# Hybrid gMLP and RG-LRU layer: spatial product in two halves with both weight parts in one matmul, another order of the v tiles, sums moved between engines

## The chip, the cores and the metric

The kernel runs on one core of a Trainium2 chip. The metric is the device time of one execution in microseconds (us). A core has a matrix engine (TensorE, PE in the profile; its weight loads are listed apart as PEld), VectorE (DVE), ScalarE (ACT), GpSimd (POOL) and SyncE (SP), which here only issues transfers. They run their own streams of instructions and wait for each other through semaphores. TensorE writes its results to PSUM, eight banks of 2 KB per partition (512 fp32 numbers); everything else lives in SBUF, 128 partitions wide.

## The reference, cut to what matters

One layer of a decoder, 1024 prompt tokens and 8 samples (T = 1032 columns), width 1024:

```
h = rmsnorm(x, norm_g) * (1 + scale) + shift
u, v, g_a, x_b, g_b, z_a, z_b = split(h @ w_in)
v = rmsnorm(v, v_norm_g)
ws = tril(w_s[g])
s = einsum('gts,bnsgc->bntgc', ws, vp) + b_s
y_a = (u * s) * silu(g_a)
xc = conv(x_b, state_conv)
a = exp(-8 r softplus(-lam)),  h_t = a_t h_{t-1} + sqrt(1 - a_t^2) (i_t xc_t)
y_b = h * silu(g_b)
merged = sigmoid(z_a) * (y_a @ w_pa) + sigmoid(z_b) * (y_b @ w_pb)
out = x + gate * (merged @ w_out);  y = rmsnorm(out, final_g)
```

The spatial product is the line with the einsum: for each of 8 groups g of 128 channels and each of 8 chunks of 128 tokens, a 128 x 128 lower-triangular matrix times v, then v's norm weight and the bias b_s. The results are wanted at fp32 accuracy.

## The kernel before, in words

**Precision.** Every fp32 operand of a matmul is split into a rounded part (hi, by a copy on ScalarE) and the rest (lo, by a subtraction on VectorE). A product is the sum of three matmuls in the fast format: hi hi, hi lo and lo hi.

**Stages.** First come the modulation vectors, h and the projection to v (`v_tile`, line 677: 24 matmuls of 512 columns for one token tile and one half of the channels, into one PSUM bank; tile 8 is the samples, 41 weight columns wide). `v_evac` (line 669) copies the bank out on VectorE and sums its squares on ScalarE. Then the program changes to four pairs of PSUM banks (`new_phase(bufs=4)`, line 1427) and runs 24 units: R i, Z i and G i for i = 0 to 7, each a block of columns of w_in against h by a Strassen scheme of seven products p1 to p7 (`seven`, line 858; 24 matmuls of 258 columns each). The order of the products is p1, p6, p5, p2, p7, p3, p4, and p1, p4, p2, p6, p5, p7, p3 in the first unit. The sums of h that this needs are made by `x_forms(kp)` (line 757): for each of four kp, four sums on GpSimd, then four more sums on VectorE, each with a split into S1 to S4. In the products' names a_, b_, c_, d_ are the pairs of banks, s_, p_, u_ the copies out of them, wf_R1p7 the split weight form of product p7 of unit R1, wt_ and raw_ its sources.

After the units come the two projections (`pa`, `pb`, 344 columns a matmul), the output projection and the last norm.

**The order of the work.** From unit 1 on, every engine runs its instructions as the program writes them (`InOrder`, line 39; nearly every row of the profile is therefore put down to line 46, in the changed kernel 45). Work beside the products stands in a table: `at(n, ...)` (line 1452) puts a step behind product n of the run, counted over all units. For group g, `spatial(g, n)` (line 1492) takes n = the first product of unit G g (five products later for the last group). Ahead of G g stands R g+1, so n - 7 is that unit's p1, n - 4 its p2 and n - 3 its p7. `v_load` at n - 9 fetches v and w_s, `v_mask`, `v_wst` and `v_scale` at n - 7 make the transposed weight wsb and the scaled v, `v_hi` at n - 6 makes vnh, `v_lo` at n - 5 makes vnl (line 1049, one subtraction on VectorE), and `sp_mm` at n - 3 (line 1066) is the spatial product: 8 token tiles of three matmuls of 128 columns. Its result sp is taken up by VectorE in `fin` (four operations of 256 columns and a small one for the samples), which waits in the list `later` until the next product's matmuls are written.

**Around the first unit.** The tiles of v's second half run on PE in the order 4, 5, 6, 8 (line 717), then the phase changes, then 7 (line 1429), the form sums of kp 0 to 2 and the first weight forms, then 3 (line 1436) and the form sums of kp 3. `do_rgconsts` (line 1134) holds a chain of small operations on 8 columns for softplus(-lam): Abs and Exp on ScalarE (`le`), then `l`, `crg` and `ncrg` on VectorE.

Of the kernel before, what the change touches and what calls it, by code (L numbers as in the profile page):

```python
# [13 lines left out]
P = 128  # L14
# [10 lines left out]
HD = 512  # L25
NF = 2
EPS = 1e-6
EVAC_PRIO = 400
C_RG = 8.0
NSLOT = 36  # L30

# [23 lines left out]
def tile_hybrid_step(  # L55
# [102 lines left out]
        A.activation(hi, src, AF.Copy)  # L158
        (eng or V).tensor_tensor(lo, src, hi.bitcast(F32), ALU.subtract)

    last_w = [None]

    def load_raw(name, shape, parts):
        raw = wst[0].tile(shape, F32, tag="raw", name=f"raw_{name}", bufs=4)
# [52 lines left out]
        )  # L217
        return rs[:rows, :n]

    crow = sml.tile([72, P], F32, tag="rows", name="crow", bufs=5)  # L220
    nc.sync.dma_start(out=crow[0:64, :], in_=c_sample.rearrange("b (k p) -> (b k) p", p=P))
    nc.sync.dma_start(out=crow[64:72, :], in_=c_prompt.rearrange("b (k p) -> (b k) p", p=P))

# [89 lines left out]
    def vec_load(eng, parts):  # L313
        a = parts[0][0]
        e = parts[-1][0] + parts[-1][1].shape[0] // P
        vrow = sml.tile([e - a, P], F32, tag="rows", name=f"vrow{a}", bufs=5)
        for off, src in parts:
            if isinstance(src, tuple):
                c0 = src[2]
                with tc.issue_after(last_w[0]):  # L320
                    for q in range(2):
                        eng.dma_start(
                            out=vrow[off - a : off - a + KT, 64 * q : 64 * q + 64],
                            in_=src[q].rearrange("(k p) -> k p", p=P)[:, c0 : c0 + 64],
                        )
                continue
            n = src.shape[0] // P
            if eng is not G:
                with tc.issue_after(last_w[0]):
                    eng.dma_start(  # L330
                        out=vrow[off - a : off - a + n, :], in_=src.rearrange("(k p) -> k p", p=P)
                    )
                continue
            eng.dma_start(
                out=vrow[off - a : off - a + n, :], in_=src.rearrange("(k p) -> k p", p=P)
            )
        return vrow, a, e
# [331 lines left out]
    def v_evac(tt, half, ps):  # L669
        st = half_tile(f"vst{tt}_{half}")[:, 0:HD]  # L670
        V.tensor_copy(st, ps)
        A.activation(junk[:, 0:HD], ps, AF.Square, accum_out=ssv[:, tt, half : half + 1])
        nc.sync.dma_start(out=vd[tt * P : (tt + 1) * P, half * HD : (half + 1) * HD], in_=st)

    vsr = slot("vsr", [P, D])[0:NS]
# [38 lines left out]
        v_evac(tt, 0, vps[tt, 0])  # L714
    v_tile(3, 0)
    v_tile(8, 0)
    for tt in (4, 5, 6):
        v_tile(tt, 1)
    v_tile(8, 1)
    vss = ctile([P, 1], "vss")  # L720
    A.activation(junk[:NS], vsr, AF.Square, accum_out=vss[:NS])
# [5 lines left out]
    V.tensor_tensor(vsr, vsr, vgb, ALU.mult)  # L727
    nc.sync.dma_start(out=chunk_v_sample[0, :, 0, :], in_=vsr)

    vst = ctile([P, KT, NS], "vst")  # L730
    vgc = ctile([P, KT], "vgc")
    w00 = ctile([P, KT], "w00")

    def spatial_consts():
        ones1 = sml.tile([1, P], F32, tag="rows", name="ones1", bufs=5)
        G.memset(ones1, 1.0)
        vgr = sml.tile([KT, P], F32, tag="rows", name="vgr", bufs=5)
        w0r = sml.tile([1, KT], F32, tag="w0r", name="w0r", bufs=1)
        with tc.issue_after(last_w[0]):
            nc.sync.dma_start(out=vgr, in_=v_norm_g[0].rearrange("(k p) -> k p", p=P))  # L740
            nc.sync.dma_start(out=w0r, in_=w_s[0, :, 0, 0:1].rearrange("g o -> o g"))
        pst = consts_pair[:, 0]
        TE.matmul(pst[:, 80 : 80 + KT], ones1, w0r, start=True, stop=True)
        for k in range(KT):
            TE.transpose(
                pst[:, k * NS : (k + 1) * NS], vsr[0:NS, k * P : (k + 1) * P], ident[0:NS, 0:NS]
            )
        TE.transpose(pst[:, 64 : 64 + KT], vgr, ident[0:KT, 0:KT])
        rg_transposes()
        A.activation(w00, pst[:, 80 : 80 + KT], AF.Copy)  # L750
        A.activation(vst, pst[:, 0:64].rearrange("p (k b) -> p k b", k=KT), AF.Copy)
        A.activation(vgc, pst[:, 64 : 64 + KT], AF.Copy)
# [4 lines left out]
    def x_forms(kp):  # L757
        a11, a21 = h[kp, 0], h[kp, 1]
        a12, a22 = h[kp + 4, 0], h[kp + 4, 1]
        f1 = slots.tile([P, 2, HT], F32, tag="s", name=f"f1_{kp}")  # L760
        f2 = slots.tile([P, 2, HT], F32, tag="s", name=f"f2_{kp}")
        f3 = slots.tile([P, 2, HT], F32, tag="s", name=f"f3_{kp}")
        for dst, a in ((f1[:, 1], a21), (f2[:, 1], a22), (f1[:, 0], a11), (f2[:, 0], a12)):
            G.tensor_tensor(dst, a[:, 0].bitcast(F32), a[:, 1].bitcast(F32), ALU.add)

        def form(name, src):
            t = slots.tile([P, 2, HT], F32R, tag="s", name=f"{name}_{kp}")
            split(t[:, 0], t[:, 1], src)
            HF[name, kp] = t

        V.tensor_tensor(f3[:, 0], f1[:, 1], f2[:, 1], ALU.add)
        form("S1", f3[:, 0])
        V.tensor_tensor(f3[:, 1], f3[:, 0], f1[:, 0], ALU.subtract)
        form("S2", f3[:, 1])
        V.tensor_tensor(f1[:, 1], f1[:, 0], f1[:, 1], ALU.subtract)
        form("S3", f1[:, 1])
        V.tensor_tensor(f2[:, 0], f2[:, 0], f3[:, 1], ALU.subtract)
        form("S4", f2[:, 0])
        HF["A11", kp], HF["A12", kp], HF["A22", kp] = a11, a12, a22
# [231 lines left out]
    def v_load(g):  # L1011
        vg = slot(f"vg{g}", [P, NT, P])
        S.dma_start(
            out=vg,
            in_=vd[:, g * P : (g + 1) * P].rearrange("(n p) c -> p n c", p=P),
        )
        wsr = aux[0].tile([P, 2, P], F32, tag="c1", name=f"wsr{g}", bufs=2)
        S.dma_start(out=wsr[:, 0], in_=w_s[0, g])
        S.dma_start(out=wsr[:, 1], in_=b_s[0, g].partition_broadcast(P))
        vn[g] = {"v": vg, "w": wsr}  # L1020

    def v_mask(g):
# [40 lines left out]

        later.append(fin)

    def sp_mm(g):
        vnl, wsr, vnh, wsb = (vn[g][k] for k in "lwhb")
        bsb = wsr[:, 1]
        ps = pair_bank(f"sp{g}")
        for n in range(NT):  # L1070
            d = ps[:, n // 4, n % 4 * P : (n % 4 + 1) * P]
            for j, (v, w) in enumerate(((vnh, 0), (vnh, 1), (vnl, 0))):
                TE.matmul(d, v[:, n, :], wsb[:, w, :], start=(j == 0), stop=(j == 2))

        def fin():
            t3 = t3s[g] = slot(f"t3_{g}")
            bv = bsb.rearrange("p (o t) -> p o t", o=1).broadcast_to([P, 2, P])
            for b in range(2):
                for q in range(2):
                    V.scalar_tensor_tensor(  # L1080
                        q4(t3)[:, 2 * b + q, 0:QP].rearrange("p (j t) -> p j t", j=2),
                        ps[:, b, q * QP : (q + 1) * QP].rearrange("p (j t) -> p j t", j=2),
                        vgc[:, g : g + 1],
                        bv,
                        ALU.mult,
                        ALU.add,
                    )
            V.scalar_tensor_tensor(
                q4(t3)[:, :, QP:QW],
                vst[:, g, :].rearrange("p (q x) -> p q x", q=4),  # L1090
                w00[:, g : g + 1],
                bsb[:, 0:1].rearrange("p (o t) -> p o t", o=1).broadcast_to([P, 4, 2]),
                ALU.mult,
                ALU.add,
            )

        later.append(fin)

# [13 lines left out]
    rgrows = []  # L1112

    def load_rgconsts():
        strow = sml.tile([64, P], F32, tag="rows", name="strow", bufs=5)
        srow = [sml.tile([96, P], F32, tag="rows", name=f"srow{j}", bufs=5) for j in range(2)]
        scv = state_conv[0].rearrange("b w (k p) -> (b w k) p", p=P)
        with tc.issue_after(last_w[0]):
            nc.sync.dma_start(
                out=strow, in_=state_rglru_h[0].rearrange("b (k p) -> (b k) p", p=P)  # L1120
            )
            for j in range(2):
                nc.sync.dma_start(out=srow[j], in_=scv[j * 96 : (j + 1) * 96, :])
            nc.sync.dma_start(out=conv_sample[0, :, 0:2, :], in_=state_conv[0, :, 1:3, :])
        rgrows.extend([strow, srow])
# [8 lines left out]
    def do_rgconsts():  # L1134
# [14 lines left out]

        lamv = vec[:, V_LAM : V_LAM + KT]  # L1150
        le = ctile([P, KT], "le")
        A.activation(le, lamv, AF.Abs)
        A.activation(le, le, AF.Exp, scale=-1.0)
        l1 = ctile([P, KT], "l1")
        V.tensor_scalar(l1, le, 2.0, None, ALU.add)
# [147 lines left out]

    def do_states(_, w):
        pso = [bank(f"pso{j}") for j in range(2)]
        orow = [sml.tile([96, P], F32, tag="rows", name=f"orow{j}", bufs=5) for j in range(2)]
        ofv = ofm[:].rearrange("p q k -> p (q k)")
        for j, (a, n) in enumerate(((0, 96), (96, 64))):
            TE.transpose(pso[j][0:n, 0:P], ofv[:, a : a + n], ident)
# [116 lines left out]
    load_rgconsts()  # L1426
    new_phase(bufs=4)
    load_unit(units[0])
    v_tile(7, 1)
    for kp in range(3):  # L1430
        x_forms(kp)
    for n in range(4):
# [59 lines left out]
    def spatial(g, n):  # L1492

        at(n - 9, v_load, g)
        at(n - 7, v_mask, g)
        at(n - 7, v_wst, g)
        at(n - 7, v_scale, g)
        at(n - 6, v_hi, g)
        at(n - 5, v_lo, g)
        at(n - 3, sp_mm, g)  # L1500

    for i in range(KT):
        recurrent(i)
# [175 lines left out]
```

## Time and profile before

| | |
|---|---|
| median of 3 runs | 971.16 us (970.68 to 972.37) |
| the profiled execution | 969.83 us |
| its span from first to last instruction | 968.1 us |
| PE busy | 944.6 us, 6639 matmuls |
| VectorE busy | 628.0 us |
| ScalarE busy | 499.8 us |
| GpSimd busy | 232.4 us |
| mean granted clock | 0.996 |

The share of busy time is an average over the span. A row of the timeline gives the start and the length of an instruction, or of neighbours of one kind that are put together, and in brackets the idle time of its engine just before it with what ended it. Matmuls overlap in the rows: the time of a stretch of them is the difference of two starts, not the sum of the lengths. The profiled execution lies 1.33 us under the median.

### The profile page before, as it was taken

How to read it: one execution, taken by the hardware profiler on the slowest of the kernel's cores; microseconds unless marked ns; L12 is line 12 of the kernel's file. 1: busy time of each engine (PE TensorE's matmuls, PEld its weight loads, DVE VectorE, ACT ScalarE, POOL GpSimd, SP SyncE). 2: the span in 40 equal slices, each digit the busy share in tenths (PEclk: the TensorE clock that was granted, in tenths of full speed). 3: DMA queues.
4: the chain of work that ended last, by engine and by line, in shares of the span. 5: the costliest groups of instructions: out<-in, count | busy, mean ns of one | idle time of the engine just before them, and what ended most of it. 6: DMA issues, size and time to landing. Idle time of an engine off the chain costs nothing. (4 is left out here: it accounts for less than half of the span.)

```text
span 968.1 us, 16680 instructions
## 1 busy us (share of the span) xinstructions
PE 944.6 (98%) x6639; PEld 883.4 (91%) x6639; DVE 628.0 (65%) x969; ACT 499.8 (52%) x809; POOL 232.4 (24%) x173
## 2 busy tenths in 40 slices
PE   7999998999999999999999999998999999999996
PEld 3777768999999999999999999998999999998785
DVE  3888878568588496685774866868443366555544
ACT  4674444784775855847747558477122223232212
POOL 1142455242232342322422523331000000000001
PEclk9999999999999999999999999999999999999998
DMA  9953112243144162341431613417775465334321
GB/s 290 288 173 110 56 51 60 61 138 114 30 137 126 40 187 60 100 131 45 137 94 38 187 51 86 144 57 273 257 270 178 172 217 188 144 99 163 110 83 50
DMA packets 126790, 125.74 MB, mean 130 GB/s; under 512 B 10374, under 2 KB 104126, under 8 KB 126704
## 3 DMA queue, kind: packets, MB, share of 16 engines
q1 hardware_dynamic: 125496, 120.44, 38.7%
q0 software_dynamic: 1216, 4.24, 1.2%
q8 instruction: 52, 0.85, 0.4%
q14 instruction: 26, 0.21, 0.1%
HBM read 93.39 MB, written 31.33 MB: 129 GB/s over the span
## 5 line engine op out<-in xcount | busy, mean ns | idle before, releaser
L46 PE MATMUL v<-wv,h 128*128 128x512 f32 x384 | 97.2, 401 | 4.3 <-DVE h L46 1.8
L46 PE MATMUL ps_pb<-ybh,pb 128*128 128x344 f32 x384 | 92.4, 323 | 3.0 <-issue 3.0
L46 PE MATMUL ps_pa<-yah,pa 128*128 128x344 f32 x384 | 91.3, 320 | 0.0
L46 PEld LDWEIGHTS v<-wv,h 128*128 128x128 f32 x384 | 69.5, 188 | 22.5 <-DVE h L46 3.5
L46 POOL TENSOR_TENSOR rs_o<-ms_o,nhalf 128x1 f32<-128x1 f32 (+1 forms) x9 | 8.0, 894 | 299.0 <-DVE ms_o L46 299.0
L46 PEld LDWEIGHTS ps_pb<-ybh,pb 128*128 128x128 f32 x384 | 67.5, 191 | 3.2 <-issue 3.2
L46 PEld LDWEIGHTS ps_pa<-yah,pa 128*128 128x128 f32 x384 | 66.4, 188 | 0.5
L46 PE MATMUL ps_pb<-ybl,pb 128*128 128x344 f32 x192 | 62.1, 323 | 0.0
L46 PE MATMUL ps_pa<-yal,pa 128*128 128x344 f32 x192 | 61.3, 319 | 0.0
L46 PE MATMUL o<-woh,mgh 128*128 128x512 f32 x128 | 50.5, 395 | 0.0
L46 PE MATMUL o<-woh,mgl 128*128 128x512 f32 x128 | 50.5, 394 | 0.0
L46 PE MATMUL o<-wol,mgh 128*128 128x512 f32 x128 | 50.4, 394 | 0.0
L46 DVE SCALAR_TENSOR_TENSOR xc<-xb,vec,xc 128x512 f32<-128x512 f32 x48 | 44.2, 920 | 0.6
L46 ACT ACT_TABLE_LOAD x34 | 43.6, 1283 | 1.4 <-PEq L1663 0.8
L46 ACT ACTIVATE mgh<-sa 128x344 fp32r<-128x344 f32 x24 | 11.7, 490 | 62.6 <-DVE sa L46 58.8
L46 DVE TENSOR_TENSOR sb<-ps_pb,sb 128x344 f32<-128x344 f32 x24 | 12.4, 516 | 47.2 <-PE ps_pb L46 46.8
L46 ACT ACTIVATE junk<-xr 128x512 bf16<-128x512 f32 (+2 forms) x19 | 11.6, 608 | 56.8 <-DVE xr L46 51.4
L46 POOL TENSOR_TENSOR wt_R<-raw_R,raw_R 128x512 f32<-128x512 f32 x8 | 16.8, 2106 | 95.4 <-DVE wf_Z4p L46 13.7
L46 PEld LDWEIGHTS ps_pb<-ybl,pb 128*128 128x128 f32 x192 | 36.7, 191 | 0.0
L46 PEld LDWEIGHTS ps_pa<-yal,pa 128*128 128x128 f32 x192 | 36.1, 188 | 0.2
L46 ACT ACTIVATE r<-rg,vec 64x516 f32<-64x516 f32 x32 | 22.0, 687 | 26.9 <-PE rg L46 26.9
L46 POOL TENSOR_TENSOR wt_R<-raw_R,wt_R 128x512 f32<-128x512 f32 x15 | 32.8, 2184 | 8.6 <-DVE wf_R2p L46 1.1
(533 smaller groups left out, 2543.7 us busy)
## 6 DMA issues: line engine op xcount, KB each, us to landing
raw_ada<-in_w_ada_dram SPq DMA_DIRECT2D x32, 256.0 KB
raw_R<-in_w_in_dram SPq DMA_DIRECT2D x16, 512.0 KB
raw_Z<-in_w_in_dram SPq DMA_DIRECT2D x16, 512.0 KB
raw_G<-in_w_in_dram SPq DMA_DIRECT2D x16, 512.0 KB
zad<-za SPq DMA_DIRECT2D x16, 258.0 KB
yad<-t SPq DMA_DIRECT2D x8, 516.0 KB
sb<-zbd SPq DMA_DIRECT2D x8, 516.0 KB
yar<-yad SPq DMA_DIRECT2D x8, 516.0 KB
```

The lines of the kernel that those rows point to most:

```text
L46: ins = f(*args, **kwargs)
```

## The change

1. The spatial product of a group is cut into two halves of four token tiles, pr = 0 behind the product at n - 4 and pr = 1 behind the one at n - 3. For each tile, the two matmuls of vnh against w_hi and w_lo become one of 256 columns, whose two results of 128 columns are written 256 columns apart in one bank; the third, vnl against w_hi, adds to the second of them. VectorE takes a half up in two operations of 2 x 256 columns in place of two of 256, the second adding to what the first wrote; for this b_s is loaded twice (8 more transfers in all).
2. The tiles of v's second half run in the order 4, 8, 5, 6, 7, all ahead of the phase change, and 3.
3. The four sums of `x_forms(3)` move from GpSimd to VectorE.
4. The first operation on `le` is written to stand behind the last sum of squares of v on ScalarE.
5. `EVAC_PRIO` (not used), the number of buffers of `rows` (5 to 4) and the place of the tile `ones1`.

```diff
 def v_evac(tt, half, ps):
-        A.activation(junk[:, 0:HD], ps, AF.Square, accum_out=ssv[:, tt, half : half + 1])
+        last_a[0] = A.activation(
+            junk[:, 0:HD], ps, AF.Square, accum_out=ssv[:, tt, half : half + 1]
+        ).ins
...
-    for tt in (4, 5, 6):
-        v_tile(tt, 1)
+    v_tile(4, 1)
     v_tile(8, 1)
...
+    for tt in (5, 6, 7):
+        v_tile(tt, 1)
...
-            G.tensor_tensor(dst, a[:, 0].bitcast(F32), a[:, 1].bitcast(F32), ALU.add)
+            (G if kp < 3 else V).tensor_tensor(
+                dst, a[:, 0].bitcast(F32), a[:, 1].bitcast(F32), ALU.add
+            )
...
-        wsr = aux[0].tile([P, 2, P], F32, tag="c1", name=f"wsr{g}", bufs=2)
+        wsr = aux[0].tile([P, 3, P], F32, tag="c1", name=f"wsr{g}", bufs=2)
         S.dma_start(out=wsr[:, 0], in_=w_s[0, g])
-        S.dma_start(out=wsr[:, 1], in_=b_s[0, g].partition_broadcast(P))
+        for j in (1, 2):
+            S.dma_start(out=wsr[:, j], in_=b_s[0, g].partition_broadcast(P))
...
-    def sp_mm(g):
+    def sp_mm(g, pr):
         vnl, wsr, vnh, wsb = (vn[g][k] for k in "lwhb")
-        bsb = wsr[:, 1]
-        ps = pair_bank(f"sp{g}")
-        for n in range(NT):
-            d = ps[:, n // 4, n % 4 * P : (n % 4 + 1) * P]
-            for j, (v, w) in enumerate(((vnh, 0), (vnh, 1), (vnl, 0))):
-                TE.matmul(d, v[:, n, :], wsb[:, w, :], start=(j == 0), stop=(j == 2))
+        wcat = wsb[:].rearrange("p a t -> p (a t)")
+        ps = pair_bank(f"sp{g}_{pr}")
+        for b in range(2):
+            parts = ps[:, b, :].rearrange("p (a j t) -> p j a t", a=2, j=2)
+            for j in range(2):
+                n = pr * 4 + b * 2 + j
+                TE.matmul(parts[:, j], vnh[:, n, :], wcat, start=True, stop=False)
+                TE.matmul(parts[:, j, 1], vnl[:, n, :], wsb[:, 0, :], start=False, stop=True)
 
         def fin():
...
+            tv = q4(t3)[:, 2 * pr : 2 * pr + 2, 0:QP]
+            vg = vgc[:, g : g + 1]
+            V.scalar_tensor_tensor(tv, ps[:, :, QP : 2 * QP], vg, bv, ALU.mult, ALU.add)
+            V.scalar_tensor_tensor(tv, ps[:, :, 0:QP], vg, tv, ALU.mult, ALU.add)
...
-        A.activation(le, lamv, AF.Abs)
+        with tc.issue_after(last_a[0]):
+            A.activation(le, lamv, AF.Abs)
...
-    v_tile(7, 1)
...
-        at(n - 3, sp_mm, g)
+        at(n - 4, sp_mm, g, 0)
+        at(n - 3, sp_mm, g, 1)
```

The first place is PE in unit R1, around the spatial product of group 0. a_R, b_R and c_R are the banks of the unit's products; the first rows are the end of p2, the b_R rows are p7, the c_R row is the start of p3. Before:

```order
L46 MATMUL a_R_2324<-h_0_734,wf_R1p_2394 128x258 x3
L46 MATMUL b_R_2325<-S_0_1399,wf_R1p_2430 128x258 x3
...
L46 MATMUL sp_2505<-wsb_2390,vnh_2401 128x128 x2
L46 MATMUL sp_2505<-wsb_2390,vnl_2436 128x128
...
L46 MATMUL c_R_2326<-S_0_1403,wf_R1p_2464 128x258 x3
```

In the changed kernel:

```order
L45 MATMUL a_R_2325<-h_0_734,wf_R1p_2395 128x258 x3
L45 MATMUL sp_0_2470<-wsb_2391,vnh_2402 128x2x128
L45 MATMUL sp_0_2470<-wsb_2391,vnl_2437 128x128
...
L45 MATMUL b_R_2326<-S_0_1399,wf_R1p_2431 128x258 x3
...
L45 MATMUL sp_1_2519<-wsb_2391,vnh_2402 128x2x128
...
```

The first matmul that reads vnl stood behind all of p7; now it is the second instruction behind p2.

The second place is VectorE in unit R2, around the subtraction that makes vnl of group 1. Before:

```order
L46 TENSOR_TENSOR vnl1_3216<-vg1_3062,vnh1_3181 128x1024
L46 TENSOR_TENSOR wf_R2p3_3244<-raw_R2_1_2866,wf_R2p3_3244 128x512
L46 TENSOR_TENSOR wf_R2p4_3277<-wt_R2_3028,wf_R2p4_3277 128x512
...
L46 SCALAR_TENSOR_TENSOR t3_1_3336<-sp1_3285,vgc_1276,wsr1_3064 128x256 x4
```

In the changed kernel:

```order
L45 TENSOR_TENSOR vnl1_3211<-vg1_3056,vnh1_3176 128x1024
L45 TENSOR_TENSOR wf_R2p3_3239<-raw_R2_1_2860,wf_R2p3_3239 128x512
L45 SCALAR_TENSOR_TENSOR t3_1_3281<-sp1_0_3244,vgc_1305,wsr1_3058 128x2x256
L45 SCALAR_TENSOR_TENSOR t3_1_3281<-sp1_0_3244,vgc_1305,t3_1_3281 128x2x256
L45 SCALAR_TENSOR_TENSOR t3_1_3281<-vst_1304,w00_1306,wsr1_3058 128x4x2
L45 TENSOR_TENSOR wf_R2p4_3285<-wt_R2_3022,wf_R2p4_3285 128x512
```

vnl keeps its place on VectorE; the operations that take up the first half of sp now stand between the lo parts of the weight forms of p3 and p4.

The third place is ScalarE ahead of the first copy out of the first unit (s1_R0). Before:

```order
L46 ACTIVATE vgc_1276<-consts_1515 128x8
L46 ACTIVATE sth_1330<-consts_1515 128x256
L46 ACTIVATE S4_3_1512<-f2_3_1493 128x516
L46 ACTIVATE s1_R0_1650<-a_R0_1595 128x516
```

In the changed kernel:

```order
L45 ACTIVATE sth_1359<-consts_1515 128x256
L45 ACTIVATE junk_100,ssv_811<-v3_1_1463 128x512
L45 ACTIVATE le_1545<-vec_101 128x8
L45 ACT_TABLE_LOAD
L45 ACTIVATE le_1545<-le_1545 128x8
L45 ACTIVATE s1_R0_1650<-a_R0_1595 128x516
```

The two operations on `le` and a table load moved directly ahead of s1_R0; the 25 operations of the chain behind them moved with them on VectorE, in among the weight splits of the first unit.

## Rows read from the trace of the kernel before

**Rows 1.** The page: busy time, share of the span and instructions of each engine.

```profile
PE 944.6 (98%) x6639; PEld 883.4 (91%) x6639; DVE 628.0 (65%) x969; ACT 499.8 (52%) x809; POOL 232.4 (24%) x173
```

**Rows 2.** Waits of PE: waiting tile, releaser: us in total, times, longest.

```profile
PE ps_pb L46 <- issue: 3.0, 1, 3.0
...
PE a_R L46 <- ACT s_R L46: 1.6, 1, 1.6
PE v L46 <- DVE vsr L46: 1.4, 1, 1.4
PE b_R L46 <- ACT u_R L46: 1.3, 1, 1.3
```

**Rows 3.** Timeline of PE from 222 us, unit R1: start, length, instruction.

```profile
223.31 3.02 PE L46 MATMUL b_R<-S,wf_R1p 128*128 128x258 f32 x24
226.17 0.33 PE L46 MATMUL sp<-wsb,vnh 128*128 128x128 f32 x2
...
228.80 3.09 PE L46 MATMUL c_R<-S,wf_R1p 128*128 128x258 f32 x24
```

**Rows 4.** Timeline of PE from 36 us: 16 matmuls of 256 columns.

```profile
39.34 0.28 PE L46 MATMUL ada<-hi_ada,scp 128*41 128x256 f32 x1
...
41.23 2.25 PE L46 MATMUL v<-wv,h 128*128 128x512 f32 x9
```

**Rows 5.** Timeline of VectorE in the same stretch of unit R1.

```profile
223.58 1.22 DVE L46 TENSOR_TENSOR vnl<-vg,vnh 128x1024 fp32r<-128x1024 f32 x1
...
229.00 1.66 DVE L46 SCALAR_TENSOR_TENSOR t<-sp,vgc,wsr 128x256 f32<-128x256 f32 x4 [0.69 <-PE sp L46]
```

**Rows 6.** Timelines of PE and VectorE in unit R7, from 612 us.

```profile
613.36 3.02 PE L46 MATMUL b_R<-S,wf_R7p 128*128 128x258 f32 x24
...
613.76 1.21 DVE L46 TENSOR_TENSOR vnl<-vg,vnh 128x1024 fp32r<-128x1024 f32 x1
```

**Rows 7.** Timelines of PE and VectorE in unit G7, group 7.

```profile
652.43 3.03 PE L46 MATMUL c_G<-S,wf_G7p 128*128 128x258 f32 x24
...
650.67 1.22 DVE L46 TENSOR_TENSOR vnl<-vg,vnh 128x1024 fp32r<-128x1024 f32 x1
```

**Rows 8.** Timelines of ScalarE, VectorE and PE from 256 us, units Z2 and R2.

```profile
256.74 0.69 ACT L46 ACTIVATE r<-rg,vec 64x516 f32<-64x516 f32 x1 [1.31 <-PE rg L46]
...
286.90 0.69 DVE L46 TENSOR_TENSOR wf_R2p<-raw_R,wf_R2p 128x512 fp32r<-128x512 f32 x1 [1.23 <-ACT wf_R2p L46]
...
288.72 1.22 DVE L46 TENSOR_TENSOR vnl<-vg,vnh 128x1024 fp32r<-128x1024 f32 x1
...
288.27 2.90 PE L46 MATMUL b_R<-S,wf_R2p 128*128 128x258 f32 x23
```

**Rows 9.** Timelines of four engines from 131 us, the way into the first unit.

```profile
153.41 3.13 PE L46 MATMUL a_R<-h,wf_R0p 128*128 128x258 f32 x24 [1.59 <-ACT s_R L46]
156.38 3.01 PE L46 MATMUL b_R<-S,wf_R0p 128*128 128x258 f32 x24
...
163.54 3.15 PE L46 MATMUL b_R<-S,wf_R0p 128*128 128x258 f32 x24 [1.29 <-ACT u_R L46]
...
152.77 0.58 ACT L46 ACTIVATE s_R<-a_R 128x516 f32<-128x516 f32 x1
...
158.76 3.48 DVE L46 SCALAR_TENSOR_TENSOR xc<-xb,vec,xc 128x512 f32<-128x512 f32 x2
...
139.85 10.58 POOL L46 TENSOR_TENSOR f<-h 128x516 f32<-128x516 f32 x4 [2.41 <-PE v L46]
```

**Rows 10.** Timelines of ScalarE and VectorE from 73 us: the chain on `le` and `l`.

```profile
74.43 1.28 ACT L46 ACT_TABLE_LOAD   x1
...
79.59 0.17 DVE L46 TENSOR_SCALAR l<-l 128x8 f32<-128x8 f32 x1
...
83.68 1.22 DVE L46 TENSOR_TENSOR l<-l,l 128x8 f32<-128x8 f32 x1
```

**Rows 11.** Busy time by window around 670 us; PEclk is the column behind POOL.

```profile
670.00:676.00 6.00, 3.00 (x12) 2.88 (x11) 5.90 (x12) 2.07 (x3) 0.00 (x0) 0.76 0.62 181
```

More of the change, by code (lines that the diff above doesn't have):

```diff
@@ L27 @@
 EPS = 1e-6
-EVAC_PRIO = 400
 C_RG = 8.0
@@ L159, in split @@
         (eng or V).tensor_tensor(lo, src, hi.bitcast(F32), ALU.subtract)
-    last_w = [None]
+    last_w, last_a = [None], [None]
     def load_raw(name, shape, parts):
@@ L218, in inv_rms @@
         return rs[:rows, :n]
-    crow = sml.tile([72, P], F32, tag="rows", name="crow", bufs=5)
+    crow = sml.tile([72, P], F32, tag="rows", name="crow", bufs=4)
     nc.sync.dma_start(out=crow[0:64, :], in_=c_sample.rearrange("b (k p) -> (b k) p", p=P))
@@ L315, in vec_load @@
         e = parts[-1][0] + parts[-1][1].shape[0] // P
-        vrow = sml.tile([e - a, P], F32, tag="rows", name=f"vrow{a}", bufs=5)
+        vrow = sml.tile([e - a, P], F32, tag="rows", name=f"vrow{a}", bufs=4)
         for off, src in parts:
@@ L734, in spatial_consts @@
     def spatial_consts():
-        ones1 = sml.tile([1, P], F32, tag="rows", name="ones1", bufs=5)
+        ones1 = sml.tile([9, 2, P], F32, tag="at", name="ones1", bufs=1)[0:1, 0]
         G.memset(ones1, 1.0)
-        vgr = sml.tile([KT, P], F32, tag="rows", name="vgr", bufs=5)
+        vgr = sml.tile([KT, P], F32, tag="rows", name="vgr", bufs=4)
         w0r = sml.tile([1, KT], F32, tag="w0r", name="w0r", bufs=1)
@@ L1064, in v_wst @@
         later.append(fin)
-    def sp_mm(g):
+    def sp_mm(g, pr):
         vnl, wsr, vnh, wsb = (vn[g][k] for k in "lwhb")
-        bsb = wsr[:, 1]
-        ps = pair_bank(f"sp{g}")
-        for n in range(NT):
-            d = ps[:, n // 4, n % 4 * P : (n % 4 + 1) * P]
-            for j, (v, w) in enumerate(((vnh, 0), (vnh, 1), (vnl, 0))):
-                TE.matmul(d, v[:, n, :], wsb[:, w, :], start=(j == 0), stop=(j == 2))
-        def fin():
[L1076 to L1095, printed above, removed]
@@ new lines, in sp_mm @@
+        wcat = wsb[:].rearrange("p a t -> p (a t)")
[6 more added lines that the diff above has]
+                TE.matmul(parts[:, j, 1], vnl[:, n, :], wsb[:, 0, :], start=False, stop=True)
+        def fin():
+            bsb = wsr[:, 1:3]
+            if pr == 0:
+                t3s[g] = slot(f"t3_{g}")
+            t3 = t3s[g]
+            bv = bsb.rearrange("p (o q) t -> p o (q t)", o=1).broadcast_to([P, 2, QP])
+            tv = q4(t3)[:, 2 * pr : 2 * pr + 2, 0:QP]
+            vg = vgc[:, g : g + 1]
+            V.scalar_tensor_tensor(tv, ps[:, :, QP : 2 * QP], vg, bv, ALU.mult, ALU.add)
+            V.scalar_tensor_tensor(tv, ps[:, :, 0:QP], vg, tv, ALU.mult, ALU.add)
+            if pr == 0:
+                V.scalar_tensor_tensor(
+                    q4(t3)[:, :, QP:QW],
+                    vst[:, g, :].rearrange("p (q x) -> p q x", q=4),
+                    w00[:, g : g + 1],
+                    bsb[:, 0, 0:1].rearrange("p (o t) -> p o t", o=1).broadcast_to([P, 4, 2]),
+                    ALU.mult,
+                    ALU.add,
+                )
@@ L1114, in load_rgconsts @@
     def load_rgconsts():
-        strow = sml.tile([64, P], F32, tag="rows", name="strow", bufs=5)
-        srow = [sml.tile([96, P], F32, tag="rows", name=f"srow{j}", bufs=5) for j in range(2)]
+        strow = sml.tile([64, P], F32, tag="rows", name="strow", bufs=4)
+        srow = [sml.tile([96, P], F32, tag="rows", name=f"srow{j}", bufs=4) for j in range(2)]
         scv = state_conv[0].rearrange("b w (k p) -> (b w k) p", p=P)
@@ L1305, in do_states @@
         pso = [bank(f"pso{j}") for j in range(2)]
-        orow = [sml.tile([96, P], F32, tag="rows", name=f"orow{j}", bufs=5) for j in range(2)]
+        orow = [sml.tile([96, P], F32, tag="rows", name=f"orow{j}", bufs=4) for j in range(2)]
         ofv = ofm[:].rearrange("p q k -> p (q k)")
```

## The prediction

> **What bounds the kernel now.** I read the page first: PE is busy for 98% of the span, VectorE for 65%, ScalarE for 52% [rows 1]. A change pays here if it takes work from PE or closes one of PE's waits, and costs if it makes PE wait. The list of PE's waits is next. Three of its larger ones lie where the change works, at the way into the first unit: 1.4 us for vsr, 1.6 for s_R and 1.3 for u_R, 4.3 us together, and 3.0 us lie at the end of the last unit [rows 2]. Between the first and the last unit PE hardly waits, so time added to PE there, work or wait, is not absorbed: it moves the end by its own length. Then the timelines, for what each matmul costs and for how late each input of the moved instructions is.
>
> **The spatial product: work.** A group's 24 matmuls of 128 columns take 226.17 to 228.80, 2.63 us or 110 ns each [rows 3]. The change makes 8 of 256 columns and 8 of 128. No row shows 256 columns with 128 weight columns; the nearest is the modulation product, 16 of 256 columns with 41 weight columns in 1.89 us, 118 ns each [rows 4]. The bounds are 110 ns (if the second 128 columns were free) and 220 ns (the two matmuls that it replaces). I take 118, the row of the same width: 8 x (118 + 110) = 1.82 us a group, 0.81 saved, 6.5 us in eight groups.
>
> A page speaks against the saving. The Trainium skill, in "TensorE: Matmul & The Clock Gate", section "Back-to-back issue gap", gives a gap of N/2.4 + 2.5 ns for a single matmul of N columns, 56 ns for 128 and 109 for 256. By that rule three short ones cost 168 ns and the new two 165, so nothing would be saved; but the rows have 110 ns for 128 columns in a stream of them, so the measurement decides.
>
> **The spatial product: place.** This is the term that decides. Before, the first matmul that reads vnl stood behind p7. Now it is the second instruction behind p2, and PE runs in order, so a vnl that is not there stops p7 and all that follows. In R1 p2 ends and p7 starts at 223.31 [rows 3]; vnl starts on VectorE at 223.58 and takes 1.22, so it ends at 224.80 [rows 5], 1.49 us behind. For group 1 it is 288.72 + 1.22 = 289.94 against 288.27, 1.67 behind [rows 8]; for group 6 613.76 + 1.21 = 614.97 against 613.36, 1.61 [rows 6]. The groups between read 1.63, 1.62, 1.63 and 1.67 in the same way; all seven make 11.3 us. The last group is five products later in its unit, and there vnl ends at 651.89, ahead of the product's end at 652.43: no wait [rows 7].
>
> Of each lag the first new matmul covers 0.12. Added is what a restart costs: 153.35, the end of s_R, to 153.41 is 0.06, and the 24 matmuls behind that wait take 2.97 us where others take 2.86 (223.31 to 226.17), 0.11 [rows 3, 9]. So the wait is 11.3 - 7 x 0.12 + 7 x 0.17 = 11.7 us.
>
> Does a later PE give vnl time to catch up? No: it would if vnl hung on something that PE's delay leaves behind. Followed back, vnl stands behind a weight form that waits for ScalarE's copy [rows 8], behind a ScalarE and VectorE chain of tanh, exp, square root and scan that begins with PE's last gate product of the unit before, `r<-rg` at 256.74 [rows 8]. Between that product and vnl nothing is added or removed, and no spatial product lies there. PE's 32 us and the other engines' 33 us from that point on both start from PE's clock, so each group loses its 1.5 us anew.
>
> What is queued behind the wait: VectorE takes up sp in order, and its first half (two operations of 512 columns; four of 256 take 1.66 us now [rows 5]) stands ahead of p4's weight form. That form is needed two products and half a spatial product later, over 6 us, and ends some 2 us behind sp; nobody waits. The second load of b_s, 8 transfers on SP, and the fewer, longer operations on VectorE lie under PE's work and cost nothing.
>
> The sum for the spatial product is 11.7 - 6.5 = +5.2 us. I keep 0.8 to either side of it for the 256-column price and the restart.
>
> **The way into the first unit.** With the samples' tile second, vsr is computed under three token tiles and the 1.4 us [rows 2] should go. The four sums on GpSimd take 10.58 us from 139.85 on [rows 9]; on VectorE, whose own sums of that size run at 0.7 us, they take 2.8, and stand no longer ahead of S4, so they come earlier. Against this: the table load of 1.28 us [rows 10] and the two small operations on `le` (0.2 us each) now run directly ahead of s_R, 1.7 us on the copy that PE waits for. The 25 operations on `l`, 0.17 us as a rule and up to 1.22 beside GpSimd's work [rows 10], come in among the weight splits, 4.5 us or more on a VectorE that is already the reason why u_R is late: the two xc operations take 3.48 us ahead of it [rows 9]. In sum VectorE has 2.8 + 4.5 us more and loses 3 us or so of slow operations beside GpSimd. Rebuilt by hand, the chain s_R, p2, p6, p5, u_R starts p7 between 160 and 166 us where it is 163.54 now [rows 9]. All three waits gone would be -4.3 us. I take +0.9, with -1.5 and +2.5 as its likely ends.
>
> A long wait costs beyond itself: the one stretch inside the units and projections where the granted clock fell, 0.76 in the mean from 670 to 676 us (some matmuls at the half level, 1.2 GHz), stands right behind PE's longest idle of 3.0 us [rows 2, 11]; the idles of 1.6 and 1.4 us have none. The new waits are of 1.5 us, so I price no such stretch into the sum.
>
> **The sum.** 5.2 + 0.9 = +6.1 us: 969.83 becomes 975.9 for an execution like the profiled one, which lay 1.33 under the median, so the median goes from 971.16 to **977 us**. A measurement of this kernel can tell 0.2%, 1.9 us, from no change.
>
> **The rivals.**
> - *vnl is there in time* (the other side). VectorE reaches vnl 1.7 us earlier, or PE is behind by that much, and only the saving is left: 971.16 - 6.5 + 0.9 = 965.6 us. It decides at p2's end: vnl must end by 0.12 us behind it. For it: VectorE sits idle for 1.23 us just ahead of the form before vnl [rows 8], so an earlier copy on ScalarE would give most of it. Against it: that copy hangs on the chain above, which the change doesn't touch, and the lag is within 0.2 us in seven groups.
> - *The first unit's waits close*. The wait for vnl is as computed, but s_R and u_R come in time: 971.16 + 5.2 - 4.3 = 972.1 us. For it: GpSimd's sums were the last into S4 and slowed VectorE beside them. Against it: the table load and the `l` chain are new exactly there.
> - *Writing two halves of a bank slows the 256-column matmul*. If it takes as long as the two that it replaces, 220 ns, nothing is saved: 971.16 + 11.7 + 0.9 = 983.8 us. No row of before has an output in two pieces; the pieces are of 128 columns in a row, which speaks against it. The Trainium skill, in "PSUM — Partial Sum Buffer", section "Specifications (TRN2)", says that any non-contiguous access pattern slows matmuls significantly, without a figure; no run here shows it yet.
> - *The waits bring half clock*. If each of seven waits were followed by such a stretch, at the 1.4 us that this one costs (0.24 of full speed missing over 6 us [rows 11]), 977.3 + 7 x 1.4 = 987.1 us. The idles of 1.6 and 1.4 us without one speak against it.
>
> **How the numbers follow.** The forecast gets 0.61: the lag is read directly, seven times, in an order that PE can't change. Its own range is 974 to 980: 0.8 for the spatial product, and -1.5 to +2.5 in place of +0.9. vnl in time gets 0.13, the first unit's waits closed 0.13 (968 to 974 with a partial wait), the slow 256-column matmul 0.08, half clock 0.05. The range 968 to 984 holds the forecast, the closed waits and the slow matmul, 0.82. Faster by more than 1.9 us (under 969.2) is the case in time and a little of the closed waits, 0.16; within 1.9 us the rest of those and the low edge of the forecast, 0.13; slower 0.71.
>
> **What would show it.** Right: the list of PE's waits has sp waiting for vnl on VectorE, seven times, about 1.5 us each; half a spatial product takes 0.9 us behind the wait; the wait for vsr is gone; s_R directly behind a table load. Wrong: no wait for vnl, or one of far less than a microsecond; 256-column matmuls 200 ns apart; PE's idle between 130 and 165 us under 2 us or over 6; windows with a granted clock well under 1 behind the new waits.

## The result, and the profile after

The changed kernel takes 976.13 us (median of 5 runs, 975.57 to 977.52) where the kernel before took 971.16 (5 runs, 969.45 to 973.46): a ratio of 1.0051, 95% interval 1.0032 to 1.0069. It is slower by half a per cent, 0.9 us off the forecast of 977 and inside its range.

The profiled execution has a span of 973.9 us, 5.8 more than before. First the page's busy times, to be held against [rows 1]:

```profile
PE 940.3 (97%) x6575; PEld 877.6 (90%) x6575; DVE 642.0 (66%) x973; ACT 499.9 (51%) x809; POOL 223.5 (23%) x169
```

PE has 4.3 us less to do and the kernel is longer: the time is in waits. The list of PE's waits in the changed kernel (us in total, times, longest), against [rows 2]:

```profile
PE sp L45 <- DVE vnl L45: 9.7, 7, 1.4
PE b_R L45 <- ACT u_R L45: 3.7, 1, 3.7
...
PE v L45 <- ACT junk L45: 1.7, 1, 1.7
PE a_R L45 <- ACT s_R L45: 1.6, 1, 1.6
PE ps_pb L45 <- DVE ybl L45: 1.5, 2, 1.1
...
PE ps_pb L45 <- DVE pb L45: 0.9, 1, 0.9
```

The first row is the forecast's main term. The wait for vsr is gone, one for the sum of squares of a v tile on ScalarE (junk), which reads a bank that PE wants next, stands in its place, u_R's wait has grown from 1.3 to 3.7, and the 3.0 us ahead of ps_pb have fallen to pieces of 0.9 and 1.5.

The timeline of PE in unit R2 of the changed kernel shows one such wait:

```profile
288.23 3.02 PE L45 MATMUL a_R<-h,wf_R2p 128*128 128x258 f32 x24
291.09 0.28 PE L45 MATMUL sp<-wsb,vnh 128*128 128x256 f32 x1
292.77 0.33 PE L45 MATMUL sp<-wsb,vnl 128*128 128x128 f32 x1 [1.40 <-DVE vnl L45]
...
293.62 3.08 PE L45 MATMUL b_R<-S,wf_R2p 128*128 128x258 f32 x24
296.54 0.28 PE L45 MATMUL sp<-wsb,vnh 128*128 128x256 f32 x1
...
297.40 0.82 PE L45 MATMUL c_R<-S,wf_R2p 128*128 128x258 f32 x5
```

and the timeline of VectorE beside it what PE waits for:

```profile
289.67 0.69 DVE L45 TENSOR_TENSOR wf_R2p<-raw_R,wf_R2p 128x512 fp32r<-128x512 f32 x1 [1.24 <-ACT wf_R2p L45]
290.28 1.29 DVE L45 TENSOR_TENSOR gr<-gr,th 128x1024 f32<-128x1024 f32 x2
291.50 1.22 DVE L45 TENSOR_TENSOR vnl<-vg,vnh 128x1024 fp32r<-128x1024 f32 x1
```

vnl ends at 292.72, 1.63 us behind p2's end at 291.09; the second matmul of sp starts 0.05 later. A half with nothing to wait for takes 296.54 to 297.40, 0.86 us for four pairs; the one that waits takes 291.09 to 293.62, 2.53 us, so 1.67 are lost.

Where the 5.8 us come from is read by the starts of the same products in both timelines (us; e6, e9 and e11 are runs told of below):

| stretch of PE | before | after | difference | e6 | e9 | e11 |
|---|---|---|---|---|---|---|
| start to p1 of R0 | 145.82 | 143.97 | -1.85 | 144.39 | 144.16 | 143.47 |
| p1 to p7 of R0 | 17.72 | 20.19 | +2.47 | 20.21 | 16.83 | 20.19 |
| p7 itself, R0 | 2.98 | 4.42 | +1.44 | 5.32 | 2.98 | 4.28 |
| R0's p3 to G7's p1 | 480.18 | 486.34 | +6.16 | 474.96 | 477.25 | 480.58 |
| G7's p1 to its last product | 20.35 | 19.28 | -1.07 | 21.17 | 19.66 | 20.36 |
| last product to ps_pb | 6.10 | 3.26 | -2.84 | 5.02 | 3.27 | 2.94 |
| ps_pb to ps_pa | 94.39 | 95.71 | +1.32 | 94.43 | 96.03 | 95.81 |

The rows make +5.63; the rest of the span adds 0.17.

### The profile page after: what moved, and what is told of

Same layout as the page of the kernel before. It is cut to its first block, busy times and chain, and to the rows that moved or that the text cites. A ratio compares the mean times of both kernels' runs of the same rounds, so it can differ in the third digit from the quotient of the medians.

```text
span 973.9 us, 16564 instructions
## 1 busy us (share of the span) xinstructions
PE 940.3 (97%) x6575; PEld 877.6 (90%) x6575; DVE 642.0 (66%) x973; ACT 499.9 (51%) x809; POOL 223.5 (23%) x169
## 5 line engine op out<-in xcount | busy, mean ns | idle before, releaser
L45 DVE SCALAR_TENSOR_TENSOR xc<-xb,vec,xc 128x512 f32<-128x512 f32 x48 | 48.2, 1005 | 0.6
L45 ACT ACTIVATE mgh<-sa 128x344 fp32r<-128x344 f32 x24 | 11.7, 490 | 63.2 <-DVE sa L45 59.3
L45 ACT ACTIVATE junk<-xr 128x512 bf16<-128x512 f32 (+2 forms) x19 | 11.6, 608 | 56.8 <-DVE xr L45 51.4
L45 POOL TENSOR_TENSOR wt_G<-raw_G,raw_G 128x512 f32<-128x512 f32 x8 | 14.0, 1755 | 92.9 <-DVE wf_G6p L45 13.9
```

Source lines behind the costliest of these rows:

```text
L45: ins = f(*args, **kwargs)
```

## The experiments

The kernel before was measured again beside each set of experiments: its medians are 970.43 (e1 to e4), 970.32 (e5 to e8) and 970.91 us (e9 to e12) where it was 971.16. The ratios below are against these. The changed kernel's 976.13 comes from the first measurement, so a difference from it can be off by up to 0.8 us.

**e1, the wait away.** Each half one product later, so that vnl has p7's time to be done.

```diff
-        at(n - 4, sp_mm, g, 0)
-        at(n - 3, sp_mm, g, 1)
+        last = g + 1 == KT
+        at(n - 3 - last, sp_mm, g, 0)
+        at(n - 2 - last, sp_mm, g, 1)
```

> The changed kernel with each half of the spatial product one product later (behind p7 and p3; the last group stays). Theory, the wait for vnl is the price: vnl ends 1.4 to 1.7 us behind p2, and p7 takes 2.86, so it is there; 7 x 1.66 us go (6.31 us from p2's end to p3 less 2.86 and 1.76), 976.1 - 11.6 = 964.5 us, and PE's list of waits has no sp. Rival, the two-piece output or the longer evacuation costs the time: no less than 974 us. Rival, another wait takes the place of it (a pair of banks not free, VectorE taking sp up late): 968 to 973 us with a new row in PE's waits between 220 and 670 us.

Measured: 969.28 us, 0.9991 of before (0.9979 to 1.0003). The wait is gone, and 6.9 us of the 11.6. The rival with another wait was right about the rest. PE in unit G1 of e1, then VectorE:

```profile
312.81 0.44 PE L45 MATMUL b_G<-S,wf_G1p 128*128 128x258 f32 x2
313.46 2.90 PE L45 MATMUL b_G<-S,wf_G1p 128*128 128x258 f32 x22 [0.21 <-DVE wf_G1p L45]
```

```profile
312.71 0.69 DVE L45 TENSOR_TENSOR wf_G1p<-raw_G,wf_G1p 128x512 fp32r<-128x512 f32 x1 [1.19 <-ACT wf_G1p L45]
```

The third matmul of p7 reads the lo part of its form, which ends at 313.40. The list gives this wait as 0.2 us, but p7 takes 316.43 - 312.81 = 3.62 in place of 2.86. This is so in the first four groups only (3.44 to 3.68, 2.9 us together; the later ones take 2.87). In the last unit PE waits another 0.7 us, for an operation of VectorE on t. Counted from the start of G1, the form's lo part ends at 10.56 us in the kernel before, 11.01 in the changed one and 12.55 in e1, and PE wants it at about 12.2. The row of the kernel before, where G1 starts at 299.56:

```profile
309.43 0.69 DVE L46 TENSOR_TENSOR wf_G1p<-raw_G,wf_G1p 128x512 fp32r<-128x512 f32 x1 [1.19 <-ACT wf_G1p L46]
```

The form hangs on the chain of xc, which VectorE runs behind what takes up sp: in e1 the second half's two operations of 0.75 us come in among xc. They also change what runs beside GpSimd. Of the six xc operations ahead of G1's p7, one takes 1.7 us in place of 0.74 in the kernel before and in e6, e9 and e11, told of below; in e1, e4 and e5 there are two such, of 1.7 and 1.8 us, and so there are in the first four groups of the changed kernel: the six take 6.42 us in place of 5.40. Each slow one overlaps GpSimd's work on the next weights. In e6 the take-up of sp stands there instead, and neither engine is slowed. VectorE and GpSimd in e1, then in e6:

```profile
297.98 1.77 DVE L45 SCALAR_TENSOR_TENSOR xc<-xb,vec,xc 128x512 f32<-128x512 f32 x1
...
297.39 1.82 POOL L45 TENSOR_TENSOR raw_G<-raw_G 128x512 f32<-128x512 f32 x1
```

```profile
298.26 0.74 DVE L45 SCALAR_TENSOR_TENSOR t<-sp,vgc,wsr 128x512 f32<-128x512 f32 x1
...
298.27 1.30 POOL L45 TENSOR_TENSOR raw_G<-raw_G 128x512 f32<-128x512 f32 x1
```

This 1.0 us is as much as the form ends later in e1 than in e6 (12.55 against 11.59); no run changes the overlap alone.

**e2, le early.** The chain on le and l back where the kernel before had it.

```diff
-        with tc.issue_after(last_a[0]):
-            A.activation(le, lamv, AF.Abs)
+        A.activation(le, lamv, AF.Abs)
```

> The changed kernel with the first operation on le not held back, so that Abs, the table load, Exp and the 25 small VectorE operations stand far ahead of the first unit again. Theory, they are why s_R and u_R are late: s_R 1.65 us earlier, the 3.70 us wait for u_R falls under 1 us, and p7 of the first unit runs at full clock (2.9 us in place of 4.4): 976.1 - 5.1 - 1.5 = 969.5 us. Rival, VectorE is late anyway by the two xc operations beside GpSimd (3.4 us): only the table load goes, about 973.5 us, and the wait for u_R stays over 2 us.

Measured: 974.69 us, 1.0039 (1.0027 to 1.0050): 1.4 us less than the changed kernel, not 6.6. The late costs did go, as the theory said: s_R's wait is 1.2, u_R's 0.7, and p7 of R0 ran at the full clock. But PE's list has a row that the changed kernel has not:

```profile
PE v L45 <- DVE h L45: 2.5, 3, 1.5
```

In the early place the l operations stand in VectorE's queue ahead of h, beside GpSimd (in e2's timeline four of them take 1.2 to 2.8 us), and PE waits for h; in the kernel before these waits were 1.8 us. In e2 they set the products of v back by 3.0 us, and the way from R0's p1 to its p3 is 4.8 us shorter than in the changed kernel: moving the chain away, which the change does, gains over half of what its new place costs. The profiled execution of e2 (977.05) is the slowest of its runs: it has another 0.8 us ahead of the first product of v and 1.5 behind a stretch of half clock in the first projection, which the changed kernel's has not.

**e3, e1 and e2 at once.** Both diffs.

> Both edits of e1 and e2 at once. Theory: they lie in different stretches and add, 976.1 - 11.6 - 6.6 = 958 us, faster than both kernels. Rival, the order of waits shifts so that one gives back what the other gains: 963 us or more.

Measured: 967.30 us, 0.9961 (0.9945 to 0.9976). The sum of the two measured gains, 8.3 us, would be 967.8: they add, and it is the two sizes that were too large.

**e4, the new product in the kernel before**, placed as in e1, with the buffers that b_s needs.

> The kernel before with the new spatial product alone, placed as in e1 (order of the v tiles, sums and le as before). Theory: the matmuls save 0.87 us in each of eight groups, 7.0 us, and nothing waits; the first projection's bank now waits for an operation of VectorE that ends about 1 us sooner: 971.2 - 7.0 - 1.0 = 963 us, or 961.7 if the stretch of half clock behind that wait goes too. Rival, the new form saves nothing: 970 us or more.

Measured: 967.24 us, 0.9958 (0.9943 to 0.9973), 3.2 us less than before. Four of its periods last 65.0 to 65.1 us (four of e1 64.9 to 65.1) and the rest 64.2, since the same form of G is late: p7 of the first four G units takes 3.1 us more together, of the 7 us that the matmuls were to save. The rival is refuted, the size of the theory too.

**e5, vnl earlier, the product where the change put it.**

```diff
         at(n - 6, v_hi, g)
-        at(n - 5, v_lo, g)
+        at(n - 6, v_lo, g)
```

> The changed kernel, spatial product where it is, but vnl made one product earlier (n - 6 in place of n - 5), ahead of the first unit product's sum b_R on VectorE, where 1.2 us of idle follow. e1 took the wait away and gained 6.9 us of 11.6: in five of its periods the product p7 of G took 3.6 us in place of 2.9, waiting for the lo part of its weight form. Theory: that came from taking sp up a product later, which delays xc; here sp is taken up early, so the full 11.6 us come, 964.5 us, and PE's list has neither vnl nor wf_G. Rival: the new take-up (four operations of 0.75 us in place of four of 0.48) makes VectorE late wherever it stands: 968 to 970 us, wf_G in the list again.

Measured: 968.17 us, 0.9976 (0.9965 to 0.9986). vnl now ends 2.1 us ahead of sp, so no wait for it; the first four periods take 64.5 to 64.8 us, the others 64.2 to 64.3. The form of G's p7 ends 12.17 us behind G1's start, just too late, and p7 takes 3.25: the rival, in a weaker form (the list of waits doesn't show wf_G). In the last group the second half waits 1.2 us for its pair of banks.

**e6, both halves behind p7**, where the whole product stood.

```diff
-        at(n - 4, sp_mm, g, 0)
+        at(n - 3, sp_mm, g, 0)
         at(n - 3, sp_mm, g, 1)
```

> The changed kernel with both halves where the whole product stood before (behind p7). No wait for vnl. Theory of place: sp is taken up as early as before but by operations that are 1.1 us longer in all, and PE is 0.9 us faster, so xc is some 1 us later against PE than before, within the 1.6 us of slack that p7's form of G had: 965 us. Rival, length alone: p7 of G waits as in e1, 968 to 970 us.

Measured: 966.75 us, 0.9957 (0.9942 to 0.9971), 9.4 us less than the changed kernel. This is the cleanest answer: from R0's p3 to G7's p1 it takes 474.96 us where the change takes 486.34, 11.4 us for seven waits, and 5.2 less than before. G's p7 waits for nothing:

```profile
313.64 3.03 PE L45 MATMUL b_G<-S,wf_G1p 128*128 128x258 f32 x24
316.51 0.64 PE L45 MATMUL rg<-xe,bdt 128*128 128x258 f32 x4
```

Its form ends 11.59 us behind G1's start. Place decides, as the theory said; what is missing to 965 us went in the last group and at the first projection (from e6's list of PE's waits):

```profile
PE ps_pb L45 <- issue: 1.9, 1, 1.9
...
PE sp L45 <- DVE t L45: 1.7, 1, 1.7
```

The profiled execution of e6, which the table shows, is the slowest of its nine runs (968.31 us): its p7 of R0 takes 0.9 us more at half clock than the changed kernel's.

**e7, the chain on le in the second unit**: the operations as three functions, called beside Z0's first three products.

```diff
-        with tc.issue_after(last_a[0]):
-            A.activation(le, lamv, AF.Abs)
...
+    at(7, lam_a)
+    at(8, lam_b)
+    at(9, lam_c)
```

> The changed kernel with the chain on le and l written into the second unit (Z0, its first three products), later than in either kernel. e2 showed that putting it early brings back PE's waits for h on VectorE (2.5 us between 76 and 100 us) and so gains 1.4 us only. Theory: its place in the change costs the table load ahead of s_R, the wait for u_R and the half clock behind it, 1.6 + 3.2 + 1.5 us, and its place before cost about 2 us for h; in Z0 VectorE is idle for over 40 per cent, so both go: 970 us. Rival, VectorE or ScalarE in Z0 is not free and the first gates come late: 973 us or more.

Measured: 973.88 us, 1.0031 (1.0016 to 1.0046), 2.3 us less than the changed kernel. Of 6.3 us expected, 4.7 are there at R0's p3 (163.83 for 168.58). Two things took part of it back: the table load made ScalarE late in Z0, and behind four short idles in the first projection a stretch of half clock came that the changed kernel has not at that place. From e7's timeline of PE, the two waits, and a window of e7 (length, busy time and instructions of PE, PEld, DVE, ACT and POOL, then the granted clock, 0.59, DMA share and GB/s):

```profile
160.85 3.14 PE L45 MATMUL b_R<-S,wf_R0p 128*128 128x258 f32 x24 [0.93 <-ACT u_R L45]
...
183.08 0.75 PE L45 MATMUL rg<-xe,bdt 128*128 128x258 f32 x4 [1.38 <-ACT ig L45]
```

```profile
682.00:686.00 4.00, 4.00 (x17) 4.00 (x17) 4.00 (x5) 2.12 (x3) 0.00 (x0) 0.59 1.10 393
```

**e8, e5 and e7 at once.**

> The edits of e5 and e7 at once. Theory: they add, 976.1 - 11.6 - 6.1 = 958.5 us, faster than both kernels by over 1 per cent. Rival: 963 us or more, if the periods or the end give part of it back.

Measured: 965.16 us, 0.9942 (0.9920 to 0.9964). The two measured gains, 8.0 and 2.3 us, would make 965.9: they add.

**e9, the best of it**: both halves behind p7, the last group as in the change, the chain on le beside the last three products of Z0.

```diff
-        at(n - 4, sp_mm, g, 0)
+        at(n - 3 - (g + 1 == KT), sp_mm, g, 0)
...
+    at(10, lam_a)
+    at(11, lam_b)
+    at(12, lam_c)
```

> The changed kernel with both halves behind p7 (the last group as in the change) and the chain on le and l in the last three products of Z0 (e7 had it in the first three, where it made ScalarE late and the second gates waited 1.4 us). From e8, 965.2 us: periods of 64.2 us as in e6 in place of 64.75, five times, 2.7 us; no wait of 1.2 us in the last group; no wait for the gates, 1.4 us: 960 us if nothing is given back. Rival: the first projection's waits bring a stretch of half clock or grow, 962 us or more.

Measured: 963.87 us, 0.9920 of before (0.9901 to 0.9940), 12.3 us less than the changed kernel and faster than both. Not 960: the chain on le still makes itself felt in Z0, as e9's list of PE's waits between 150 and 660 us shows.

```profile
PE rg L45 <- ACT ig L45: 1.6, 1, 1.6
PE a_R L45 <- ACT s_R L45: 1.2, 1, 1.2
PE b_R L45 <- ACT u_R L45: 0.8, 1, 0.8
PE b_Z L45 <- DVE p_Z L45: 0.7, 1, 0.7
```

The first and the last are new against the changed kernel, 2.3 us, which is what e9 has more than e6 from R0's p3 to G7's p1.

**e10, the last sums back on GpSimd.**

```diff
-            (G if kp < 3 else V).tensor_tensor(
-                dst, a[:, 0].bitcast(F32), a[:, 1].bitcast(F32), ALU.add
-            )
+            G.tensor_tensor(dst, a[:, 0].bitcast(F32), a[:, 1].bitcast(F32), ALU.add)
```

> The changed kernel with the four sums of the last x_forms back on GpSimd. Theory: their place is worth little, since the table load and the l chain decide when s_R and u_R come: 975 to 978 us, with VectorE free of 2.8 us of sums but slowed beside GpSimd. Rival, the move is what keeps S4 in time: S4 and s_R come 2 us or more later, 978 us or more.

Measured: 977.10 us, 1.0059 (1.0036 to 1.0081), within 1 us of the changed kernel. The waits change places (3.6 us for a sum of squares ahead of the constants, none for s_R, 1.5 for u_R), R0's p3 starts at 168.92 in place of 168.58. The move is worth little either way.

**e11, the old product in the changed kernel.**

```diff
-        at(n - 4, sp_mm, g, 0)
-        at(n - 3, sp_mm, g, 1)
+        at(n - 3, sp_mm, g)
```

(with `sp_mm` as before)

> The changed kernel with the spatial product of before (24 matmuls of 128 columns behind p7, four operations of 256 columns), so the other three parts alone. Theory: from the first unit's p3 to the last unit's p1 the change takes 6.2 us more than before, and 0.9 us less in the last group, so 976.1 - 5.3 = 970.8 us: the rest of the change is worth nothing either way, its gains (h, the first projection's bank) and losses (u_R, half clock) being equal. Rival, the spatial product is not the whole loss: 973 us or more.

Measured: 972.03 us, 1.0007 (0.9996 to 1.0019). The other parts together cannot be told from no change, so the spatial product is the loss: 976.13 - 972.03 = 4.1 us by the medians and 5.4 between the two profiled executions, either side of the forecast's 5.2.

**e12, the order of the v tiles as before**: 4, 5, 6, 8, the phase change, 7, then 3.

> The changed kernel with the tiles of v in the order of before (4, 5, 6, 8, phase change, 7, then 3). Theory: the order is worth nothing by itself, since the wait for vsr (1.4 us) goes and one of 1.7 us for a pair of banks comes: 975.5 to 977.5 us. Rival, it gains or loses by over 1.9 us, through the chain of vsr on VectorE or the rotation of the banks up to the first projection.

Measured: 975.50 us, 1.0045 (1.0027 to 1.0063). The wait for vsr is back with 1.4 us, that for junk is gone; the order is worth nothing by itself.

## Why the prediction was right, and where it was not

**The wait for vnl** (forecast 11.7 us, 1.67 a group): shown, with 1.67 us lost in R2. The seven lags were read as 1.49, 1.67, 1.63, 1.62, 1.63, 1.67 and 1.61 us, and measured as 1.41, 1.63, 1.62, 1.67, 1.67, 1.66 and 1.67, none in the last group. Taking it away behind p7 gives 11.4 us (e6). That a later PE gives vnl no time was the point on which it hung: each period of the changed kernel loses the same, 65.9 us where e6 has 64.2 and the kernel before 65.0.

**The matmuls** (forecast 1.82 us a group): 0.86 a half, 1.72 a group, so 0.91 saved where 0.81 was forecast; the periods of e6 are 0.8 us shorter than those of the kernel before (64.2 for 65.0). The rival of the output in two pieces is refuted: 256 columns and 128 take 0.86 / 4 = 0.215 us as a pair, below the 118 + 110 ns of [rows 3, 4]. Against it stood the Trainium skill, "PSUM — Partial Sum Buffer", section "Specifications (TRN2)", that a non-contiguous pattern slows matmuls significantly; pieces of 128 columns, 256 apart, don't here. The forecast also held against the rule that it took from the Trainium skill, "TensorE: Matmul & The Clock Gate", section "Back-to-back issue gap": by it 0.02 us a group would have been saved. That section gives the rule for a matmul by itself and says that it is too low for a stream of short ones, so the page did not speak against the saving as the prediction has it.

**"Nobody waits" for the longer take-up on VectorE**: true in the changed kernel only because the waits for vnl give VectorE time. e1, e4 and e5, which have no such wait, pay 0.2 to 0.8 us at G's p7 in each of the first four groups. The slack of its form was 1.6 us; in e1 the form is 2.0 us later, and 1.0 of that is the second slow xc beside GpSimd, which the forecast did not see. The last three groups have it too and are in time (11.1 us in e1); why is open. The rival "vnl in time" was priced at 965.6; e5, where vnl is in time, gives 968.2.

**The way into the first unit** (forecast +0.9, likely ends -1.5 and +2.5): +2.06 (the first three rows of the table), inside these ends. p7 starts at 164.16 where it was 163.54, 0.62 later and near the forecast; the other 1.44 are p7 itself. But the terms were not those of the forecast. Missed altogether was a gain: without the l operations PE no longer waits 1.8 us for h (the early phase is 1.85 us shorter; e2 brings the wait back). The gain of vsr's 1.4 us did not come, since a wait of 1.7 for junk stands in its place. And u_R ends 0.63 us later for a PE that is there 1.8 us sooner, so that its wait is 3.7 us; with the chain elsewhere it is 0.7 to 0.9 (e2, e7, e9). The chain on VectorE has 23 operations, not the 25 that the prediction counts, and with the one of 1.16 us they take 4.9 us, near its 4.5. PE's idle between 130 and 165 us is 1.73 + 1.65 + 3.70 = 7.1 us, over the 6 that the prediction named as a sign of being wrong. On ScalarE and VectorE of the changed kernel:

```profile
149.36 0.20 ACT L45 ACTIVATE le<-vec 128x8 f32<-128x8 f32 x1
149.58 1.28 ACT L45 ACT_TABLE_LOAD   x1
150.87 0.21 ACT L45 ACTIVATE le<-le 128x8 f32<-128x8 f32 x1
150.99 0.58 ACT L45 ACTIVATE s_R<-a_R 128x516 f32<-128x516 f32 x1
```

```profile
152.41 0.17 DVE L45 TENSOR_SCALAR l<-le 128x8 f32<-128x8 f32 x1
...
157.68 1.16 DVE L45 TENSOR_SCALAR crg<-l 128x8 f32<-128x8 f32 x1
...
159.42 3.44 DVE L45 SCALAR_TENSOR_TENSOR xc<-xb,vec,xc 128x512 f32<-128x512 f32 x2
162.78 0.69 DVE L45 TENSOR_TENSOR b_R<-b_R,s_R 128x516 f32<-128x516 f32 x1
```

And the step "I price no such stretch into the sum" failed: it held for the waits for vnl, behind which the granted clock stayed at 1.00, but u_R's wait was longer than any in the sum, and p7 behind it took 4.42 us in place of 2.98. PE and the windows (granted clock 0.90 and 0.76):

```profile
164.16 4.58 PE L45 MATMUL b_R<-S,wf_R0p 128*128 128x258 f32 x24 [3.70 <-ACT u_R L45]
168.58 3.03 PE L45 MATMUL c_R<-S,wf_R0p 128*128 128x258 f32 x24
```

```profile
160.00:165.00 5.00, 1.30 (x8) 1.10 (x8) 4.69 (x5) 1.49 (x3) 2.31 (x2) 0.90 0.00 0
165.00:170.00 5.00, 5.00 (x34) 5.00 (x34) 1.92 (x4) 0.75 (x2) 0.00 (x0) 0.76 0.46 128
```

**The end of the units**, on which the forecast put nothing, gained 1.5 us (-2.84 and +1.32). The first matmul of the first projection needs a bank of the units. In the kernel before VectorE was still reading it (the last operation on b_G of unit G7, which ends at 673.05), and PE went on 0.10 behind:

```profile
672.36 0.69 DVE L46 TENSOR_TENSOR t<-b_G,t 128x516 f32<-128x516 f32 x1
...
673.15 0.62 PE L46 MATMUL ps_pb<-ybh,pb 128*128 128x344 f32 x1 [3.00 <-issue]
```

In the changed kernel it starts at 677.46, ahead of VectorE's reads of c_G (678.77) and b_G (679.86), so its bank was free. The order of the v tiles turns the rotation of the banks, as the seventh tile no longer takes a pair: e12, which differs from the changed kernel in that alone, has a wait of 2.3 us there, right behind the read of c_G, and e11, with the old product and the new order, has none. It is not the order alone: e5, e6 and e8 keep the new order and wait 1.9 us, also right behind the read of c_G, and what turns the rotation there is open. The 3.0 us [rows 2] become waits for the operands:

```profile
677.46 0.43 PE L45 MATMUL ps_pb<-ybh,pb 128*128 128x344 f32 x1 [0.15 <-ACT pb L45]
...
678.91 0.58 PE L45 MATMUL ps_pb<-ybh,pb 128*128 128x344 f32 x2 [0.86 <-DVE pb L45]
```

That the sum came out at 6.1 where the span shows 5.8 is thus partly luck: the spatial product was as forecast (+6.16 - 1.07 = +5.1 us), the way in 1.2 us worse, the end 1.5 better.

## What to carry to other kernels

An instruction that is moved ahead on an in-order engine brings with it the time at which its last operand is ready; read that operand's end against the new place, period by period, and ask whether the chain that makes it is started by the same engine (then the wait repeats) before counting what the instruction saves. A gain on the engine that bounds the kernel uses up the slack of the next one: look for the work that now stands closest to its due time, here a weight form with 1.6 us, and for what an operation that is moved will run beside on the other engines. And a change in the order in which buffers are taken from a pool can turn the rotation of those that come later; see which reader the next user of a bank waits for.

## What the runs showed of the hardware beyond what was expected

A matmul of 256 columns whose output lies in two pieces of 128 ran no slower than one with its output in one piece (0.86 us for four of them with four of 128). An xc operation of VectorE took 0.74 to 0.76 us where it overlapped nothing of GpSimd; those of 1.7 to 1.8 all overlapped it, but some that did took 0.74. The take-up of sp, which reads PSUM, took 0.74 beside a sum of GpSimd (e6).

Half clock, the lower of TensorE's two levels (a granted clock of 0.51 from 673 to 676 us in the kernel before, 0.50 from 164 to 168 in e5) stood behind each single idle of PE, but for the wait at each kernel's start, of 3.0 us (before), 3.6 (e10, e12) and 3.7 (changed kernel, e1, e5, e6, e11) and cost the product behind it 1.3 to 2.4 us; none stood behind those of 1.4 to 1.7 in the units. In between it was there or not: behind 1.9 and 2.3 us yes in e6, e8 and e12, no in e4 and e5. e4 alone has it from 14.5 to 17.8 us (0.50), behind idles of 0.4 to 0.6. The four idles of 0.2 to 1.1 us in the first projection brought it in e2, e7 and e10, and not in the changed kernel, e1, e3, e9 and e11. What tells these apart is not settled by the runs; it is worth 1.3 to 2.4 us of any result here.
